# S5 input projections ahead of their blocks, stored in their final layout, and four MLA gates in the last heads

## The chip, the cores and the metric

One core of one Trainium2 chip runs the whole program. The metric is the device time of one execution in microseconds (us). TensorE multiplies matrices, VectorE (DVE) and GpSimd (POOL) compute elementwise, ScalarE (ACT) evacuates and casts, and SyncE (SP) issues every DMA of this kernel. Each engine works through its own queue strictly in order and waits there on semaphores of the others.

## What is computed

The reference runs two decoder layers over 512 tokens of width 1024 in float32. Each layer normalises its input, projects it once, runs three causal mixers on slices of that projection, and merges them by gates:

```python
h = rms_norm(x, g_pre)
p = h @ w_in       # SSD z, x/B/C, dt | S5 input u, gate z_b | MLA q latent, kv latent, rope key, gate z_c | 3 merge gates
A = ssd_branch(...) @ w_a       # Mamba-2 SSD in chunks of 128
B = s5_branch(...) @ w_b        # complex diagonal SSM, 64 groups of 16 channels, state 64
C = mla_branch(...) @ w_c       # 16 heads, q rank 512, kv rank 256, rotary key
merged = sum(sigmoid(gate_i) * branch_i)
x = x + rms_norm(merged @ w_o, g_post)
```

The S5 branch takes u = the S5 slice of p, 1024 channels by 512 tokens, through

```python
bu = einsum('gph,bsgh->bsgp', bb, uf)            # input matrix per group
x  = associative_scan(complex_combine, (abar, bu))
y  = Re(einsum(c, x)) + d_skip * uf
```

## The kernel before

Activations are held transposed, channels on the partitions and the 512 tokens in the free dimension. Every float32 product is made of three matmuls of split operands (upper times upper, lower times upper, upper times lower). `dense` (L108) does one projection of 128 output channels: `weight` (L92) loads a 512 KB tile wf on SP (L102, two buffers), ScalarE casts it to its upper half wh (L66), VectorE or, in the MLA stage for every third tile, POOL subtracts to get the lower half wl (L78, L81), and 24 matmuls of 128x512 follow (L116, L117, L119). `proj` is `dense` on a tile of w_in; UB + b is the S5 input of block b, GT + 8 * i + m the merge gate of branch i, tile m.

A layer (`layer`, L980) has two stages. In the MLA stage (`mla`) the latents are projected and normalised (`normed`, with row sums and copies through TensorE, L231 and L237, and a power on POOL that gives rs_r), and a loop over 16 heads makes queries, keys and values for the heads ahead (`make_q`, `make_k`, `make_v`), scores of head h + 1 (`attend_qk`) and the values of head h. `make_k` also copies the rotary parts of queries, qh and ql, by DMA (L550). Beside it runs the preparation of S5, a Python generator (`s5_prep`) that `fill(n)` advances by n steps after each head: 2 after even heads, 3 after odd ones, one after each of two points near the latents.

`s5_prep` goes through eight blocks of eight groups. `block(b)` projects the block, ScalarE evacuates it with the tokens reversed inside their eights (L321), SP stores it to DRAM (ud, L322), loads it back in eight pieces so that 128 partitions hold offset and channel (puf, L325), and stores that again as u2 (printed as u, L329), for the S5 stage later. `front(b, s)` makes the filters of two groups on POOL (pv, pw, and a store odr, L365); `back(b, s)`, one step later, transposes pw (pm, L377), multiplies it with the split input (pM, L386 and L387), makes pk from pv (L395) and stores kpad (L404) and, at the end of the block, the chunk sums mo (msd, L406). The tiles pu, puf and pmo share one tag with two buffers.

In the mix stage (`mix`) two gates of branch 2 are made, the attention outputs are scaled by rows copied with a selector (L1014, L1026) and split, and eight merges of the MLA branch (one gate and one product with w_c each, gates two ahead) run beside `s5_scan`, 63 sequential steps of four small VectorE operations (L896 to L899). Then come the SSD part, the S5 blocks and the output.

The order on each engine is not written by hand: the program is handed to a scheduler that takes the order in which the code is written as priority, fits instructions into each engine's queue by its own timeline and may pull them forward where their operands and buffers allow.

## Time and profile before

| | us |
|---|---|
| median of 3 runs | 1980.36 |
| lowest, highest | 1975.66, 1982.38 |
| the profiled execution | 1977.92 |
| its span | 1976.1 |
| TensorE busy in it | 1870.3 (95%) |
| VectorE busy | 1420.3 (72%) |
| ScalarE busy | 914.2 (46%) |
| POOL busy | 631.9 (32%) |

In layer 0 the MLA stage runs from about 25 to 390 us, mix from there to about 1025; in layer 1 the MLA stage runs from about 1045 to 1366. The engine shares are means over stages with different limits, so the tables of stretches are read before them. "Idle" is the time for which an engine stood before an instruction, with the instruction that released it. The granted clock is a share of TensorE's full 2.4 GHz; 0.5 is its lower level, 1.2 GHz.

### The profile page before, as it was taken

What the parts mean: (1) busy time and instruction counts of PE and PEld (TensorE: products, weight loads), DVE (VectorE), ACT (ScalarE), POOL (GpSimd) and SP (SyncE); (2) the same over time, 40 slices, a digit from 0 to 9 for tenths busy, and PEclk for the clock granted to TensorE, in tenths of its full rate; (3) what the DMA queues carried; (4) which work ended last, traced back from release to release, by engine and by line L of the source; (5) the groups of instructions that cost most, each with busy time, mean ns of one, the idle gap of its engine ahead of it and who ended that gap; (6) DMA issues with size and microseconds to landing.
All of it is one profiled execution on the core that took longest, in us unless ns stands there. A gap on an engine that the chain in (4) does not pass through costs nothing.

```text
span 1976.1 us, 28153 instructions
## 1 busy us (share of the span) xinstructions
PE 1870.3 (95%) x9880; PEld 1528.1 (77%) x9880; DVE 1420.3 (72%) x2882; ACT 914.2 (46%) x1647; POOL 631.9 (32%) x679
## 2 busy tenths in 40 slices
PE   7898999899999989999998989999999999999998
PEld 5687777687877868888876877776878887788887
DVE  6866566799999857744578566667999996776443
ACT  4355455522555545533332555554235663554331
POOL 1746656201233201201118465661013331012010
PEclk9898998899999999999997999998999999999999
DMA  5343333322321266345233334343332224662541
GB/s 158 94 114 94 108 114 103 119 92 84 128 65 64 75 187 182 92 152 167 90 83 90 111 93 122 100 128 96 96 130 75 74 76 113 183 174 86 171 128 43
DMA packets 136253, 219.99 MB, mean 111 GB/s; under 512 B 39856, under 2 KB 79408, under 8 KB 135600
## 3 DMA queue, kind: packets, MB, share of 16 engines
q1 hardware_dynamic: 136112, 218.19, 37.1%
q8 instruction: 78, 1.28, 0.3%
q14 instruction: 63, 0.52, 0.1%
HBM read 182.08 MB, written 31.33 MB: 108 GB/s over the span
## 4 chain that ended last, share of the span: by engine, by line
PE 60%; DVE 22%; DMA 9%; ACT 3%; issue 2%; POOL 2%; SPq 2%; DVEq 0%; ACTq 0%; POOLq 0%
PE mm L116 15%; PE mm L117 14%; PE mm L119 14%; DMA wf<-in_w_in 3%; DVE wl L78 3%; DVE keep L69 3%; PE mm L61 2%; PE mm L62 2%; PE mm L63 2%; PE aux L61 1%; DVE tmp L69 1%; DVE ms L899 1%; PE aux L62 1%; PE aux L63 1%; DVE sc_t L896 1%
## 5 line engine op out<-in xcount | busy, mean ns | idle before, releaser
L116 PE MATMUL mm<-hh,wh 128*128 128x512 f32 (+1 forms) x1232 | 499.5, 405 | 11.5 <-ACT wh L66 8.0
L66 ACT ACTIVATE wh<-wf 128x1024 fp32r<-128x1024 f32 (+1 forms) x294 | 291.3, 994 | 440.2 <-PE mm L117 227.2
L117 PE MATMUL mm<-hl,wh 128*128 128x512 f32 (+1 forms) x1232 | 492.0, 399 | 0.0
L78 DVE TENSOR_TENSOR wl<-wf,wh 128x1024 fp32r<-128x1024 f32 (+1 forms) x243 | 294.8, 1218 | 188.1 <-ACT wh L66 154.3
L119 PE MATMUL mm<-hh,wl 128*128 128x512 f32 (+1 forms) x1232 | 314.9, 393 | 1.9 <-DVE wl L78 1.9
L116 PEld LDWEIGHTS mm<-hh,wh 128*128 128x128 f32 (+1 forms) x1232 | 236.5, 192 | 72.2 <-ACT wh L66 11.6
L117 PEld LDWEIGHTS mm<-hl,wh 128*128 128x128 f32 (+1 forms) x1232 | 236.2, 192 | 48.5 <-issue 0.5
L119 PEld LDWEIGHTS mm<-hh,wl 128*128 128x128 f32 (+1 forms) x1232 | 228.2, 188 | 52.6 <-DVE wl L78 2.3
L81 POOL TENSOR_TENSOR mg<-mg,tmp 128x512 f32<-128x512 f32 x32 | 77.7, 2431 | 458.1 <-DVE tmp L78 240.5
L81 POOL TENSOR_TENSOR wl<-wf,wh 128x1024 fp32r<-128x1024 f32 (+1 forms) x51 | 108.9, 2135 | 302.6 <-PE mm L119 209.3
L116 PE MATMUL mm<-ah,wh 128*128 128x512 f32 x512 | 200.3, 393 | 0.0
L117 PE MATMUL mm<-al,wh 128*128 128x512 f32 x512 | 199.9, 391 | 0.0
L119 PE MATMUL mm<-ah,wl 128*128 128x512 f32 x512 | 127.6, 390 | 0.0
L116 PEld LDWEIGHTS mm<-ah,wh 128*128 128x128 f32 x512 | 96.2, 188 | 21.4 <-ACT pkf L66 0.7
L117 PEld LDWEIGHTS mm<-al,wh 128*128 128x128 f32 x512 | 96.1, 188 | 20.9 <-issue 1.0
L119 PEld LDWEIGHTS mm<-ah,wl 128*128 128x128 f32 x512 | 95.7, 188 | 19.6
L617 DVE CUSTOM_DVE_ANT_0 sc<-aux,cmask 128x128 f32<-128x128 f32 (+3 forms) x128 | 60.9, 485 | 63.5 <-PE aux L63 62.5
L66 ACT ACTIVATE sc<-sc,nm 128x128 f32<-128x128 f32 (+3 forms) x128 | 70.4, 554 | 13.3 <-DVE nm L73 13.2
L81 POOL TENSOR_TENSOR pv<-pq,ar 128x288 f32<-128x288 f32 x64 | 49.1, 789 | 77.2 <-PE pk L395 68.7
L69 DVE SCALAR_TENSOR_TENSOR keep<-mm,cw,keep 128x511 f32<-128x511 f32 (+2 forms) x96 | 71.1, 740 | 2.0 <-ACT keep L66 1.5
L66 ACT ACTIVATE tmp<-mm 128x512 f32<-128x512 f32 x76 | 44.8, 592 | 56.2 <-PE mm L63 31.5
L81 POOL TENSOR_TENSOR pw<-pbb,ar 128x256 f32<-128x256 f32 x64 | 51.0, 799 | 41.8 <-PE pm L377 41.6
(346 smaller groups left out, 4002.8 us busy)
## 6 DMA issues: line engine op xcount, KB each, us to landing
wf<-in_w_in SPq DMA_DIRECT2D x156, 512.0 KB, 3.6
odr<-pv SPq DMA_DIRECT2D x64, 128.0 KB, 2.0
wf<-in_w_c SPq DMA_DIRECT2D x16, 512.0 KB, 3.4
wf<-in_w_a SPq DMA_DIRECT2D x16, 512.0 KB
wf<-kpad SPq DMA_DIRECT2D x128, 64.0 KB, 6.4
wf<-odr SPq DMA_DIRECT2D x16, 512.0 KB, 7.1
wf<-in_w_glu SPq DMA_DIRECT2D x16, 512.0 KB, 3.4
wf<-in_w_b SPq DMA_DIRECT2D x16, 512.0 KB, 3.8
```

Of the source, the lines that this page charges most:

```text
L61: mm(out, ah, bh, start=start, stop=False)
L62: mm(out, ah, bl, start=False, stop=False)
L63: mm(out, al, bh, start=False, stop=stop)
L66: self.nc.scalar.activation(out, in_, func, **kw)
L69: self.nc.vector.scalar_tensor_tensor(out, in0, s, in1, op0, op1)
L78: self.nc.vector.tensor_tensor(out, a, b, op)
L81: self.nc.gpsimd.tensor_tensor(out, a, b, op)
L116: mm(ps[:m], wh[:, o(i)], bh, start=i == 0, stop=False)
L117: mm(ps[:m], wh[:, o(i)], bl, start=False, stop=False)
L119: mm(ps[:m], wl[:, o(i)], bh, start=False, stop=i == k - 1)
L617: nc.vector.tensor_tensor_reduce(out=sc, in0=ps[:, :n], in1=self.cmask[:, 512 - n:512], op0=ALU.add, op1=ALU.max, scale=1.0, scalar=-3.0e3 ...
L896: nc.vector.tensor_tensor(t1, sc1, s, ALU.mult)
```

## The change

The S5 projection becomes a function of its own, `s5_u`, with the evacuation and eight stores that put the tile in DRAM in the layout u2, in runs of 64 floats. Two blocks are projected right behind the latents (`inputs(2)`), one in each odd head behind `make_k` and `make_v`. In `s5_prep` the block is no longer projected; `load(b)` fetches it with one load (puf, now L328) together with three small loads of its matrices, one quarter of a block ahead. pu, puf and pmo get tags of their own. There is one step less per block, so `fill` is 2 after every head. The first four gates of branch 2 are made in heads 12 to 15, into four buffers of a tag gk, for which a smaller `dynamic_dma_scratch_size` leaves the space; the call in `mix` then finds them made.

```diff
+    def s5_u(self, l, pp, b):
+
+        ps = self.proj(l, UB + b)
+        u = pp.tile([P, 512], F32, name="pu", tag="pu").rearrange("p (j c) -> p j c", j=8)
+        self.act_(u[:, ::-1], ps.rearrange("p (c j) -> p j c", j=8))
+        for g in range(8):
+            self.nc.sync.dma_start(
+                self.u2[b, :, 64 * g:64 * g + 64].rearrange("(j h) c -> h j c", j=8), u[16 * g:16 * g + 16],
+            )
...
-        def block(b):
-
-            ps = self.proj(l, UB + b)
-            u = pf("pu").rearrange("p (j c) -> p j c", j=8)
-            self.act_(u[:, ::-1], ps.rearrange("p (c j) -> p j c", j=8))
-            nc.sync.dma_start(ud[b].rearrange("g h j c -> (g h) j c"), u)
-            uf = pf("puf")
-            for j in range(8):
-                nc.sync.dma_start(
-                    uf[16 * j:16 * j + 16].rearrange("h (g c) -> h g c", g=8),
-                    ud[b, :, :, j].rearrange("g h c -> h g c"),
-                )
-            nc.sync.dma_start(u2[b], uf)
+        def load(b):
+
+            uf = pt("puf", [P, 512], 2)
+            nc.sync.dma_start(uf, u2[b])
             g8 = slice(8 * b, 8 * b + 8)
-            x1, x2 = (pt(n, [P, 8, 2, 16]) for n in ("bc1", "bc2"))
+            x1, x2 = pt("bc1", [P, 8, 2, 16]), pt("bc2", [P, 8, 2, 16], 2)
...
-                keep["mo"] = pf("pmo").rearrange("p (g c) -> p g c", g=8)
+                keep["mo"] = pt("pmo", [P, 512], 2).rearrange("p (g c) -> p g c", g=8)
...
-        todo = None
+        todo, nxt = None, load(0)
         for b in range(8):
-            blk = block(b)
-            yield
+            blk = block(b, *nxt)
             for s in range(4):
...
+                if s == 2 and b < 7:
+                    nxt = load(b + 1)
                 yield
...
-        t = self.tmp()
+        t = self.tp.tile([P, 512], F32, name="gk", tag="gk", bufs=4) if i == 2 and m < 4 else self.tmp()
...
             cq, ckv = latent(CQ, 4), latent(CKV, 2)
+            inputs(2)
             cq = normed(*cq, qn, "cq")
...
+                if h % 2 == 1:
+                    inputs(1)
                 if h < 15:
                     pr[h + 1] = self.attend_qk(mp, q[h + 1], kt[(h + 1) % 2], h + 1)
                 values(h)
-                fill(3 if h % 2 else 2)
+                self.gates_ahead(l, 2, max(0, h - 11))
+                fill(2)
...
-            self.gates, self.gdone = {}, [0, 0, 0]
-            self.gates_ahead(l, 2, 2)
+            self.gates_ahead(l, 2, 4)
...
-    nc = bacc.Bacc("TRN2", target_bir_lowering=False, num_devices=1)
+    nc = bacc.Bacc("TRN2", target_bir_lowering=False, num_devices=1, dynamic_dma_scratch_size=1024)
```

What this does to the order on the engines is shown at three places. The first is SP's queue near heads 4 and 5 of layer 0, before the change: the round trip of block 2 (puf, u), the copies qh and ql, the stores of the block before (kpad, msd) and of the filters (odr), and the weight load of a projection (wf).

```order
L325 DMA puf<-ud_582 16x8x64 x8
L550 DMA qh<-rrh 32x512
L550 DMA ql<-rrl 32x512
L550 DMA qh<-rrh 32x512
L550 DMA ql<-rrl 32x512
L329 DMA u_581<-puf 128x512
L404 DMA kpad_578<-pkf 16x128 x4
L406 DMA msd_580<-pmo 2x64x512
L365 DMA odr_579<-pv_2144 128x2x128 x2
L102 DMA wf<-in_w_in 128x1024
```

The same place in the changed program:

```order
L246 DMA u_393<-pu 16x8x64 x8
L102 DMA wf<-in_w_ukv 128x512
L557 DMA qh<-rrh 32x512 x2
L557 DMA ql<-rrl 32x512 x2
L328 DMA puf<-u_393 128x512
L102 DMA wf<-in_w_in 128x1024 x2
L409 DMA kpad_579<-pkf 16x128 x4
```

The weight loads now stand ahead of the stores of kpad and odr, and behind the eight stores of the tile and one reload.

The second place is POOL's queue in the prologue of layer 0, before the change: the last instructions ahead of rs_r, which the normalisation of the q latent waits for (pw and pv are filter products, pbs and pu factors of them, wl the lower half of a weight).

```order
L81 TENSOR_TENSOR pw_1183<-pbb_766,ar 128x256
L81 TENSOR_TENSOR pw_1193<-pbb_766,ar 128x256
L81 TENSOR_TENSOR wl<-wf,wh 128x1024
L81 TENSOR_TENSOR pv_1334<-bc_815,ai 128x288
L81 TENSOR_TENSOR pbs<-pbs,pu_819 128x128
L81 TENSOR_TENSOR rs_r<-rs_v,mhalf 128x4
```

The last instructions ahead of rs_r in the changed program:

```order
L81 TENSOR_TENSOR pw_1261<-pbs,ai 128x256
L81 TENSOR_TENSOR pv_1259<-bc_854,ai 128x288
L81 TENSOR_TENSOR pv_1258<-pv_1258,pv_1259 128x288
L81 TENSOR_TENSOR pv_1421<-bc_854,ai 128x288
L81 TENSOR_TENSOR pv_1258<-pv_1258,pv_1421 128x288
L81 TENSOR_TENSOR pu_1443<-bc_1297,p_fis 128x128
L81 TENSOR_TENSOR rs_r<-rs_v,mhalf 128x4
```

Counted from the first product with p_fr, 15 instructions of POOL stood ahead of rs_r, and now stand 24, among them the filters of a whole further quarter block and no lower half of a weight.

The third place is TensorE's queue at the seam of MLA and mix in layer 0, before the change: copies with the selector (aux from r2 and sel), the third gate (mm_4651 from hh) and the first merge (mm_4619 from al).

```order
L119 MATMUL mm_4651<-hh_110,wl_4647 128x512 x3
L1026 MATMUL aux_4331<-r2_4287,sel_4294 128x512
L119 MATMUL mm_4651<-hh_110,wl_4647 128x512 x3
L1026 MATMUL aux_4338<-r2_4287,sel_4294 128x512
L119 MATMUL mm_4651<-hh_110,wl_4647 128x512 x2
L117 MATMUL mm_4619<-al_4300,wh_4614 128x512
```

The same place in the changed program, where mm_4676 and mm_4708 are the first two merges:

```order
L1044 MATMUL aux_4381<-r2_4344,sel_4351 128x512
L116 MATMUL mm_4676<-ah_4356,wh_4671 128x512
L116 MATMUL mm_4708<-ah_4356,wh_4703 128x512
L1044 MATMUL aux_4388<-r2_4344,sel_4351 128x512
L117 MATMUL mm_4676<-al_4357,wh_4671 128x512
```

The gate between the copies is gone, and matmuls of the first two merges stand there.

## Rows read from the trace of the kernel before

All rows are of the one profiled execution; times are microseconds from the start of its span.

**Rows 1.** Busy time of each engine in four stretches: the two MLA stages without their ends (105 to 360 and 1085 to 1340), and in layer 0 the first part of the mix stage (402 to 480) and the SSD part (480 to 700). Columns: stretch, its length, then busy us and instructions of PE, PEld, DVE, ACT and POOL, then the granted TensorE clock as a share of full speed, the DMA share and GB/s.
```profile
105.00:360.00 255.00, 237.81 (x1329) 197.79 (x1328) 159.45 (x359) 139.93 (x331) 146.18 (x200) 0.94 0.37 109
...
402.00:480.00 78.00, 78.00 (x351) 63.85 (x349) 74.97 (x259) 18.96 (x23) 4.79 (x2) 1.00 0.30 95
480.00:700.00 220.00, 213.49 (x1137) 173.09 (x1136) 197.31 (x326) 115.11 (x187) 64.36 (x44) 0.98 0.28 86
1085.00:1340.00 255.00, 239.14 (x1341) 198.00 (x1341) 159.68 (x361) 139.70 (x332) 153.97 (x206) 0.95 0.39 110
```

**Rows 2.** The same view for the stretches in the two MLA stages in which the granted clock falls to about half.
```profile
181.00:191.00 10.00, 6.66 (x26) 5.61 (x26) 6.77 (x14) 6.03 (x14) 7.59 (x12) 0.51 0.36 113
325.00:335.00 10.00, 9.26 (x30) 7.62 (x31) 8.11 (x20) 4.97 (x11) 6.71 (x12) 0.51 0.40 125
...
1126.00:1130.00 4.00, 3.94 (x12) 2.91 (x12) 1.76 (x6) 3.28 (x11) 0.00 (x0) 0.58 0.59 185
1167.00:1174.00 7.00, 4.18 (x16) 3.52 (x17) 5.88 (x14) 4.46 (x11) 6.35 (x10) 0.55 0.32 94
1307.00:1314.00 7.00, 6.32 (x24) 5.10 (x24) 6.01 (x16) 3.58 (x8) 3.19 (x7) 0.54 0.45 125
```

**Rows 3.** The timeline of TensorE at the places where it stood idle in the MLA stages. Columns: start, duration, engine, line, operation, tiles and shape, and in brackets the idle time just before, with what ended it.
```profile
183.68 0.69 PE L377 MATMUL pm<-ident,pw 128*128 128x128 f32 x2 [3.68 <-ACT pkf L66]
...
241.84 0.33 PE L61 MATMUL aux<-kh,qh 96*128 96x128 f32 x1 [3.38 <-DMA qh<-rrh]
...
325.27 0.47 PE L386 MATMUL pM<-pu,pmh 128*128 128x128 f32 x1 [1.57 <-ACT pmh L66]
...
1124.84 0.33 PE L386 MATMUL pM<-pu,pmh 128*128 128x128 f32 x1 [1.84 <-DVE pu L78]
...
1168.61 0.66 PE L377 MATMUL pm<-ident,pw 128*128 128x128 f32 x2 [2.41 <-ACT pkf L66]
...
1305.60 0.33 PE L386 MATMUL pM<-pu,pmh 128*128 128x128 f32 x1 [2.56 <-ACT pmh L66]
```

**Rows 4.** The timeline of ScalarE at the casts of a weight tile into its upper half (the same columns).
```profile
182.13 1.06 ACT L66 ACTIVATE wh<-wf 128x1024 fp32r<-128x1024 f32 x1 [4.68 <-DMA wf<-in_w_in]
...
322.58 1.06 ACT L66 ACTIVATE wh<-wf 128x1024 fp32r<-128x1024 f32 x1 [1.55 <-DMA wf<-in_w_in]
...
1302.91 1.06 ACT L66 ACTIVATE wh<-wf 128x1024 fp32r<-128x1024 f32 x1 [1.90 <-DMA wf<-in_w_in]
```

**Rows 5.** The timeline of SP's queue ahead of the weight load whose cast is the first row of group 4. The durations are the time that SP takes to issue.
```profile
169.41 0.46 SPq L329 DMA_DIRECT2D u<-puf  x1
169.92 1.84 SPq L404 DMA_DIRECT2D kpad<-pkf  x4
171.81 0.57 SPq L406 DMA_DIRECT2D msd<-pmo  x1
172.47 0.93 SPq L365 DMA_DIRECT2D odr<-pv  x2
173.51 1.10 SPq L102 DMA_DIRECT2D wf<-in_w_in  x1
```

**Rows 6.** The list of DMA issues of the whole program: how many, KB each, and the median us from issue to landing.
```profile
wf<-in_w_in SPq DMA_DIRECT2D x156, 512.0 KB, 3.6
...
odr<-pv SPq DMA_DIRECT2D x64, 128.0 KB, 2.0
...
puf<-ud SPq DMA_DIRECT2D x128, 32.0 KB, 2.0
```

**Rows 7.** The timeline of SP's queue ahead of the copies of head 8's query.
```profile
234.43 0.41 SPq L322 DMA_DIRECT2D ud<-pu  x1
...
237.05 2.71 SPq L325 DMA_DIRECT2D puf<-ud  x6
...
239.86 1.20 SPq L550 DMA_DIRECT2D qh<-rrh  x2
```

**Rows 8.** The prologue of the two MLA stages: timeline rows of POOL (from the first product with p_fr to rs_r in layer 0, the first product in layer 1), timeline rows of PE (the row sums and copies of L237 in both layers, and two later waits in layer 1), and last the page's group of the filter products pv (busy us, mean ns of one, idle before).
```profile
62.77 1.45 POOL L81 TENSOR_TENSOR pbb<-bc,p_fr 128x128 f32<-128x128 f32 x1 [2.18 <-DVE p_fr L78]
...
74.50 1.02 POOL L81 TENSOR_TENSOR rs_r<-rs_v,mhalf 128x4 f32<-128x4 f32 x1
...
1047.72 0.46 POOL L81 TENSOR_TENSOR pbb<-bc,p_fr 128x128 f32<-128x128 f32 x1 [1.78 <-DVE p_fr L78]
...
78.61 1.94 PE L237 MATMUL aux<-tmp,ones 128*128 128x512 f32 x2 [3.44 <-DVE tmp L73]
...
1056.19 1.13 PE L237 MATMUL aux<-tmp,ones 128*128 128x512 f32 x2 [1.83 <-DVE tmp L73]
...
1062.94 0.69 PE L377 MATMUL pm<-ident,pw 128*128 128x128 f32 x2 [2.86 <-POOL pw L81]
...
1079.39 0.42 PE L387 MATMUL pM<-pu,pml 128*128 128x64 f32 x1 [4.22 <-DVE pml L78]
...
L81 POOL TENSOR_TENSOR pv<-pq,ar 128x288 f32<-128x288 f32 x64 | 49.1, 789 | 77.2 <-PE pk L395 68.7
```

**Rows 9.** Groups of VectorE's instructions from 395 to 450 us: one of the four operations of a scan step (busy us, mean ns of one, idle before).
```profile
L899 DVE TENSOR_TENSOR ms<-ms,sc_t 128x64 f32<-128x64 f32 x37 | 10.4, 282 | 0.9
```

**Rows 10.** The timeline of TensorE at the seam of MLA and mix in layer 0: the last copy with the selector and the first matmul of the gate after the first two merges.
```profile
390.54 0.50 PE L1026 MATMUL aux<-r,sel 64*128 64x512 f32 x1
...
401.89 0.39 PE L116 MATMUL mm<-hh,wh 128*128 128x512 f32 x1
```

More of the change, by code (lines that the diff above doesn't have):

```diff
@@ L303, in s5_prep @@
         d = lambda nm, shape: self.dr.tile(shape, F32, name=f"{nm}{l}")
-        kpad, odr, msd, u2 = d("kpad", [16, 64, 240]), d("odr", [P, 64, P]), d("msd", [2, 64, 2, 32, 64]), d("u2", [8, P, 512])
-        ud = d("ud", [8, 8, 16, 8, 64])
+        kpad, odr, msd, u2 = d("kpad", [16, 64, 240]), d("odr", [P, 64, P]), d("msd", [2, 64, 2, 32, 64]), self.u2
         nc.sync.dma_start(kpad[:, :, 0:112], zero.unsqueeze(1).broadcast_to([16, 64, 112]))
@@ L310, in s5_prep @@
         et = self.gt
-        pf = lambda nm: pp.tile([P, 512], F32, name=nm, tag="pf", bufs=2)
         bbp = [pt(f"pbb{i}", [P, 8, 32]) for i in range(2)]
@@ L334, in block @@
             nc.sync.dma_start(x2[64:128], a["s5_bc"][l, 0:64, g8])
+            return uf, x1, x2
+        def block(b, uf, x1, x2):
+            g8 = slice(8 * b, 8 * b + 8)
             b1, b2, c1, c2 = x1[:, :, 0], x2[:, :, 0], x1[:, :, 1], x2[:, :, 1]
             fb = lambda x: x[:, g8].unsqueeze(2).broadcast_to([P, 8, 16])
-            u1, bs, q1 = (pt(n, [P, 8, 16]) for n in ("pu1", "pbs", "pq1"))
+            u1 = pp.tile([P, 8, 16], F32, name="pu1", tag="pv2")
+            bs, q1 = (pt(n, [P, 8, 16]) for n in ("pbs", "pq1"))
             bb = bbp[b % 2][:, :, 0:16]
@@ L478, in merge, with mla @@
         self.gt(mg, mg, g, ALU.add)
-    def mla(self, l, fill):
+    def mla(self, l, fill, inputs):
         nc, tc, a = self.nc, self.tc, self.a
@@ L987, in layer, with inputs @@
         self.yc = []
+        self.gates, self.gdone = {}, [0, 0, 0]
         with ExitStack() as pst:
             pp = pst.enter_context(tc.tile_pool(name=f"prep{l}", bufs=1, reuse_waits="tile", side="right"))
+            self.u2 = self.dr.tile([8, P, 512], F32, name=f"u2{l}")
+            todo_u = list(range(8))
+            def inputs(n):
+                for b in todo_u[:n]:
+                    self.s5_u(l, pp, b)
+                del todo_u[:n]
             prep = self.s5_prep(l, pp)
@@ L994, in fill @@
                     next(prep, None)
-            self.mla(l, fill)
+            self.mla(l, fill, inputs)
             fill(99)
```

## Prediction

> **What bounds the kernel now.** I read the table of stretches first, because the share of busy time over the whole program hides that its stages have different limits. In the MLA stage TensorE has matmuls in flight for 237.81 of 255 us in layer 0 and 239.14 of 255 in layer 1, at a granted clock of 0.94 and 0.95, while VectorE is busy 159 us and SP's queue moves data at a share of 0.37 to 0.39 [rows 1]. So TensorE sets the pace there, and what is lost is lost in two ways: it stands still, or it runs at 1.2 instead of 2.4 GHz after it stood still. In the first part of the mix stage (402 to 480 us) TensorE is never idle and VectorE is busy 74.97 of 78 us; in the SSD part (480 to 700) TensorE has 6.5 us free and VectorE 22.7 [rows 1]. VectorE has slack in MLA, little in mix.
>
> Then I looked for the places where the clock falls, and what TensorE waited for just ahead of them. At 181 to 191 us the granted clock is 0.51, at 325 to 335 again 0.51, and in layer 1 0.58 at 1126, 0.55 at 1167, 0.54 at 1307 [rows 2]. Ahead of them TensorE idles for 3.68, 1.57, 1.84, 2.41 and 2.56 us [rows 3], in four of the five for ScalarE, in whose queue the cast of a weight tile is waiting: the row of that cast at 182.13 had idled 4.68 us for the DMA of its weights, the one at 322.58 1.55 us, the one at 1302.91 1.90 us [rows 4]. SP shows why the weights were late: their issue at 173.51 stands behind the S5 store at 169.41, four kpad stores, the msd store and two odr stores, which SP issues first [rows 5]. From that issue to the cast are 182.13 - 173.51 = 8.6 us, although such a transfer takes 3.6 at the median [rows 4 to 6]: the weights are issued late, and then travel behind what was issued ahead of them. The S5 round trip through DRAM (ud out, eight puf in, u out) thus costs little itself; what costs is that it and the stores of the block before stand in SP's strictly ordered queue in front of weights.
>
> **The change part by part.** TensorE executes the same number of matmuls. What goes are 16 ud stores, 128 puf loads and 16 u stores; what comes are 128 stores of the evacuated tile and 16 reloads, and each tile is stored a head or more ahead of its use.
>
> *Late weights (gain).* In the changed order weights, the copies and the reload follow on the S5 stores, and kpad and odr come behind them. Each place costs its idle time plus what the low clock loses: at 181 us 3.68 + 10 x (1 - 0.51) = 8.6; at 1167 2.41 + 7 x 0.45 = 5.6; at 325 1.57 + 4.9 = 6.5; at 1307 2.56 + 7 x 0.46 = 5.8 [rows 2, 3]. All together 26.5 us. The first two hang on the queue order that goes, and I take them whole (14.2). At the other two the weights' own wait is shorter (1.55 and 1.90), and with it gone the next thing in ScalarE's queue can be late too, so I take half (6.1). Sum 20.3 us, bounds 7 and 26.5.
>
> *Late S5 input (gain).* At 1124.84 the pM matmuls wait 1.84 us for the split of the reloaded input, and 4 us at 0.58 follow [rows 2, 3]: 1.84 + 1.7 = 3.5 us. The reload now goes out one quarter of a block ahead of the block's first use, from data stored long before. I take 3.5, bounds 0 and 3.5.
>
> *Query copies behind more issues (loss).* Head 8's copies (idle of 3.38 us at 241.84 [rows 3]) were issued 239.86 - 234.43 = 5.4 us after the ud store [rows 7]. Now eight stores stand there, at 2.71 / 6 = 0.45 us per issue 3.6 us, then the landing of the last store (2.0 as for odr, also a store of short pieces [rows 6]; the weight load behind it is issued in its shadow) and the reload (0.46 [rows 5]): 6.1 us, or 0.7 later. With as much at a lowered clock that is about 1 us in each layer: 2 us, bounds 0 and what the rival below gives. A 256 B-piece store to DRAM has no row here; the nearest are the 256 B loads and the 512 B odr stores, both 2.0 [rows 6].
>
> *Prologue.* The normalisation of the q latent needs rs_r from POOL, which runs in order. Before, rs_r starts at 74.50, behind POOL work that began with p_fr's product at 62.77, and TensorE's row 78.61 follows 3.1 us after rs_r ends, having idled 3.44 [rows 8]. In the changed order 24 POOL instructions, from that product on, stand ahead of it: 15 of 0.79 and 8 of 0.46 are 15.5 us [rows 8], near 17 with a square over 512 columns, so rs_r would start near 80.0, 5.5 later. The second S5 projection at the latents is 24 matmuls more ahead of that point, 5.3 us by the rows' 0.222 (78 us with 351 matmuls [rows 1]). The two cancel: the idle time stays near 3.6. In layer 1 the same 17 us after 1047.72 give 1064.7 for rs_r and 1069 for the row that was at 1056.19: 12.8 later, with 5.3 of cover and thus 7.5 us more idle time. Against that, TensorE's waits of 2.86 us for pw and 4.22 for pml [rows 8] fall away, as POOL has by then gone through these filters. I charge 2 us, bounds a gain of 3 and a loss of 8.
>
> *Two projections per layer from mix into MLA.* One more S5 projection at the latents and one more gate in heads 12 to 15 (two of the four gates already ran in heads 13 and 14, since the scheduler had pulled them there). For TensorE alone that is neutral: 10.7 us more in one stage and 10.7 less in the other. But VectorE's scan of 252 small operations (0.28 us each [rows 9]) is worked off beside mix's projections, about 16 operations for each. At the start of SSD 89 of them are left in the order before and 106 after: 17 x 0.27 = 4.7 us more VectorE work there per layer, with 22.7 us free in 220 [rows 1]. I take half, 2.3 per layer, so 4.7 us; bounds 0 and, if nothing of the removed 10.7 us comes out of mix, 21.
>
> *Seam between MLA and mix.* Gate 2's matmuls stood between the eight sel copies. The last copy is at 390.54 and the next gate at 401.89 [rows 10], 11.4 us, which is the two merges in between (2 x 5.3) and hardly more. Without gate 2, the copies are paced by VectorE's multiplication and split, so that they end hardly earlier while 5.3 us of cover are gone; the merges fill it in part, as the order shows. I charge 1 us per layer, 2 us; bounds a gain of 3 and a loss of 6.
>
> Sum: 20.3 + 3.5 - 2 - 2 - 4.7 - 2 = 13.1 us off. The profiled execution took 1977.92 us (a span of 1976.1 and 1.8 around it), which gives 1964.8. The median of the runs lies 2.4 above that execution, so I forecast **1967 us**.
>
> **The rivals.** *All stalls go.* The late weights at their upper bound, 26.5, the late input 3.5, the 3.38 us idle time at 241.84 with about 1.7 at a lowered clock also gone (5), prologue and seam at their gains (3 + 3), nothing lost on VectorE: 41 us off, 1937, or 1939 by the median. For it speaks that all these waits have SP's queue behind them; against it that the prologue's waits are POOL's and that VectorE has little slack in mix.
>
> *The stalls only move.* With weights early, the copies or ScalarE's evacuations can be the next to be late, at the same places. Then half of the 14.2 us remains, 7, against the losses of 10.7: 3.7 slower than the profiled run, 1982 and 1984 by the median, which is no change. *The two projections are paid twice:* VectorE keeps mix as long as it is (74.97 of 78 busy) while MLA grows by 2 x 10.7 = 21. Then 23.8 - 21 - 6 = -3, also 1984 by the median. The free 22.7 us in the SSD part speak against it.
>
> *Slower: the short-piece stores.* The reload puf waits for the last of eight stores, and SP holds everything behind it: copies at heads 8 and 12, in both layers four places. If a store takes 2.0 us to land, the cost is the 2 us above. Beyond that each further microsecond is idle time at four places, and a stretch at the low clock comes on top, at 1167 us 7 x 0.45 = 3.2 [rows 2]. From about 3.5 us of landing it decides: each place then loses 1.5 + 3.2 us, and 4 x 4.7 = 19 against 13 is the bound to slower. At the full price of the place at 181 us, 8.6 us each, it is 34 - 13 = 21 us slower: 1999; the middle of the two is 27, 1977.9 - 13.1 + 27 + 2.4 = 1994. For it speaks that the pieces are half as long as odr's; against it the puf loads, which have 256 B pieces and land in 2.0 [rows 6].
>
> The Trainium skill (DMA: Bandwidth & Descriptors, Specifications) says that line rate needs transfers of at least 512 B and that shorter ones make the engines read, modify and write. By that the stores would be the slow ones and the 1994 of this rival the forecast. No run here shows a 256 B store, and the 256 B loads landing in 2.0 agree with no such loss on the reading side.
>
> That the change doesn't do what it says is excluded: the built order has the second projection at the latents and the gates in the last heads.
>
> **How the numbers follow.** A measurement of this kernel can tell about 0.3% from no change, 6 us, so faster is under 1974.4 and slower over 1986.3. The forecast (1955 to 1974) gets 0.43, all stalls gone 0.12, stalls moved 0.17, paid twice 0.10, short-piece stores 0.18. Faster is 0.43 + 0.12 = 0.55, the same 0.27, slower 0.18. The range reaches from the upper part of the all-gone case, 1942, to the lower half of the store rival, 1990; what lies outside is about half of either, 0.15.
>
> **What would show it.** Right: no wait of over 3 us for weights in ScalarE's casts near heads 4 and 12, a clock of 0.97 or more over the MLA stretches, and MLA longer by less than 10.7 us per layer while the mix stage is shorter by 5 to 10. Wrong: SP waiting for u2 stores longer than 2.5 us with TensorE idle for copies behind it; rs_r late in layer 1 with TensorE idle for over 8 us; VectorE over 95% busy in the SSD part with TensorE waiting for it; or idle times of the same sum that name other releasers.

## The result and the profile after

| | us |
|---|---|
| after, median of 4 runs (1998.40 to 2002.53) | 2001.51 |
| before, beside it, median of 4 runs (1975.66 to 1982.38) | 1978.69 |
| ratio, with its 95% interval | 1.0120 (1.0099 to 1.0141) |
| span of the profiled execution, before and after | 1976.1 and 2000.4 |

The kernel became slower by some 23 us, where a gain was forecast. The range of 1942 to 1990 does not hold the time.

Where the 24.3 us of the two spans lie is seen by three marks in each layer, read from the timelines: TensorE's first score matmul (aux from kh, qh), its last copy with the selector, and SP's first load of w_o. Differences are taken before rounding.

| from, to | before | after | difference | of it, moved work | rest |
|---|---|---|---|---|---|
| layer 0: start to first score | 111.7 | 119.6 | +7.9 | +5.3 | +2.6 |
| first score to last copy | 278.8 | 282.8 | +4.0 | 0 | +4.0 |
| last copy to w_o | 476.7 | 476.7 | 0 | -5.3 | +5.3 |
| layer 1: w_o to first score | 224.9 | 232.4 | +7.5 | +5.3 | +2.2 |
| first score to last copy | 277.5 | 280.7 | +3.3 | 0 | +3.3 |
| last copy to w_o | 469.8 | 471.7 | +1.9 | -5.3 | +7.2 |

What moved is one S5 projection from the heads to the latents, and the third and fourth gate out of the seam and the mix stage into the heads (5.3 us each by the forecast's 0.222 us for a matmul). So the heads get one projection less and one gate more than they and the seam had together, and mix one gate less. The rests are 4.8 us in the prologues, 7.2 in heads and seam, 12.5 in mix.

The same stretches as in [rows 1], after:

```profile
105.00:360.00 255.00, 233.55 (x1280) 195.21 (x1281) 163.30 (x353) 134.33 (x318) 152.43 (x203) 0.93 0.36 100
402.00:480.00 78.00, 78.00 (x350) 63.34 (x350) 74.43 (x269) 19.36 (x22) 4.85 (x2) 1.00 0.28 88
480.00:700.00 220.00, 209.50 (x1117) 169.50 (x1115) 195.59 (x349) 112.26 (x183) 64.50 (x43) 0.99 0.25 80
1085.00:1340.00 255.00, 231.40 (x1271) 192.00 (x1271) 169.15 (x361) 135.27 (x321) 157.58 (x211) 0.93 0.35 97
```

The MLA stretches have less TensorE work in them than before and no better clock (0.93 against 0.94 and 0.95). The idle times of [rows 3] are gone from their places, and others stand elsewhere. TensorE's timeline after:

```profile
86.88 1.12 PE L237 MATMUL aux<-tmp,ones 128*128 128x512 f32 x2 [3.15 <-DVE tmp L73]
...
181.52 0.47 PE L61 MATMUL aux<-kh,qh 96*128 96x128 f32 x1 [4.47 <-DMA qh<-rrh]
...
395.42 0.79 PE L1044 MATMUL aux<-r,sel 64*128 64x512 f32 x1 [3.88 <-DVE keep L78]
...
1096.90 0.48 PE L391 MATMUL pM<-pu,pmh 128*128 128x128 f32 x1 [6.04 <-ACT pmh L66]
...
1175.39 0.47 PE L61 MATMUL aux<-kh,qh 96*128 96x128 f32 x1 [4.20 <-DMA qh<-rrh]
```

The low clock follows them as it did the old ones:

```profile
180.00:187.00 7.00, 5.48 (x25) 4.69 (x25) 1.61 (x6) 1.01 (x2) 0.23 (x1) 0.52 0.51 174
388.00:402.00 14.00, 8.00 (x16) 4.24 (x17) 9.67 (x24) 4.64 (x9) 0.00 (x0) 0.64 0.54 175
1173.00:1180.00 7.00, 4.61 (x22) 3.77 (x22) 0.69 (x1) 1.01 (x2) 1.57 (x3) 0.53 0.67 198
```

ScalarE still waits for weights. These are its waits for the loads of weight tiles in the stretches 105 to 360 and 1085 to 1340 us (total, times, longest), after:

```profile
ACT wh L66 <- DMA wf<-in_w_in: 9.5, 4, 4.5
ACT wh L66 <- DMA wf<-in_w_ukv: 5.6, 1, 5.6
...
ACT wh L66 <- DMA wf<-in_w_in: 6.9, 2, 4.5
ACT wh L66 <- DMA wf<-in_w_ukv: 5.6, 2, 5.2
ACT wh L66 <- DMA wf<-in_w_uq: 1.8, 1, 1.8
```

And before:

```profile
ACT wh L66 <- DMA wf<-in_w_in: 7.5, 3, 4.7
ACT wh L66 <- DMA wf<-in_w_uq: 1.0, 1, 1.0
...
ACT wh L66 <- DMA wf<-in_w_in: 6.0, 2, 4.1
ACT wh L66 <- DMA wf<-in_w_uq: 6.0, 1, 6.0
```

That is 29.4 us after and 20.5 before. Two of the casts after:

```profile
181.30 0.63 ACT L66 ACTIVATE wh<-wf 128x512 fp32r<-128x512 f32 x1 [5.62 <-DMA wf<-in_w_ukv]
...
297.96 1.06 ACT L66 ACTIVATE wh<-wf 128x1024 fp32r<-128x1024 f32 x1 [4.46 <-DMA wf<-in_w_in]
```

The load for the second one was issued 2.70 us behind an msd store, and its cast began 6.89 us after its issue, where such loads land in 3.5 us at the median:

```profile
288.37 0.57 SPq L411 DMA_DIRECT2D msd<-pmo  x1
290.47 0.38 SPq L370 DMA_DIRECT2D odr<-pv  x1
291.07 0.33 SPq L102 DMA_DIRECT2D wf<-in_w_in  x1
```

The place at 181 us can be followed back. SP's queue ahead of the copies that TensorE waited for:

```profile
163.94 0.57 SPq L411 DMA_DIRECT2D msd<-pmo  x1
165.32 1.72 SPq L409 DMA_DIRECT2D kpad<-pkf  x4
167.15 0.38 SPq L370 DMA_DIRECT2D odr<-pv  x1
172.65 0.36 SPq L331 DMA_DIRECT2D bc<-in_s_bc  x1
173.05 0.53 SPq L332 DMA_DIRECT2D bc<-in_s_bc  x1
173.64 0.59 SPq L333 DMA_DIRECT2D bc<-in_s_bc  x1
174.33 3.88 SPq L246 DMA_DIRECT2D u<-pu  x8
178.33 0.36 SPq L102 DMA_DIRECT2D wf<-in_w_ukv  x1
```

SP issues nothing from 167.5 to 172.65; the load bc of L331, whose tile has one buffer, waits for POOL, which has to have read the tile's last content. POOL's timeline at that time:

```profile
165.34 0.47 POOL L81 TENSOR_TENSOR pbb<-pbb,pu 128x128 f32<-128x128 f32 x1
171.93 0.11 POOL L378 MEMSET pmo<- 128x8 f32 x1 [6.12 <-DMA msd<-pmo]
172.00 0.62 POOL L81 TENSOR_TENSOR pu<-bc,p_fi 128x128 f32<-128x128 f32 x1
```

POOL stands 6.12 us ahead of a memset of 0.11 us, until the msd store that was issued at 163.94 has landed, 8 us later. Then pu frees bc, SP loads it, issues the eight stores for 3.88 us, and only then the copies. Over layer 0's MLA stage that memset's group reads, after and before:

```profile
L378 POOL MEMSET pmo<- 128x8 f32 x6 | 0.7, 112 | 31.1 <-DMA msd<-pmo 25.4 <-DVE mx L627 5.7
```
```profile
L373 POOL MEMSET pmo<- 128x8 f32 x7 | 0.8, 113 | 6.9 <-DMA msd<-pmo 4.7 <-DMA wf<-in_w_uq 1.8 <-DMA kpad<-pkf 0.4
```

And SP's waits for POOL's filters, ahead of the odr stores, rose from the second row's value to the first's (total, times, longest):

```profile
SPq L370 <- POOL pv L81: 67.8, 19, 7.9
```
```profile
SPq L365 <- POOL pv L81: 26.8, 13, 8.5
```

The tag of its own is what let the scheduler pull the memset up to the store of the block that had used the tile. At the seam VectorE stands for a small load that now lies behind the last msd store in SP's queue, and the copies with the selector behind VectorE:

```profile
394.61 0.17 DVE L75 TENSOR_SCALAR e_zc<-alog 128x16 f32<-128x16 f32 x1 [3.61 <-DMA alog<-in_a_log]
```

### The profile page after: what moved, and what is told of

Its sections match the earlier page's. It is cut to its first block, busy times and chain, and to the rows that moved or that the text cites. A ratio compares the mean times of both kernels' runs of the same rounds, so it can differ in the third digit from the quotient of the medians.

```text
span 2000.4 us, 28062 instructions
## 1 busy us (share of the span) xinstructions
PE 1872.1 (94%) x9880; PEld 1531.8 (77%) x9880; DVE 1413.7 (71%) x2882; ACT 913.6 (46%) x1647; POOL 632.1 (32%) x679
## 4 chain that ended last, share of the span: by engine, by line
PE 54%; DVE 22%; DMA 13%; ACT 3%; issue 3%; SPq 3%; POOL 2%; DVEq 0%; ACTq 0%; POOLq 0%
PE mm L116 13%; PE mm L117 13%; PE mm L119 11%; DVE wl L78 4%; DVE keep L69 3%; DMA msd<-pmo 2%; PE mm L61 2%; DMA wf<-in_w_in 2%; PE mm L63 2%; PE mm L62 2%; DVE sc_t L906 2%; DVE ms L909 2%; DMA wf<-odr 2%; PE aux L61 2%; ACT wh L66 1%
## 5 line engine op out<-in xcount | busy, mean ns | idle before, releaser
L116 PE MATMUL mm<-hh,wh 128*128 128x512 f32 (+1 forms) x1232 | 493.2, 400 | 10.5 <-DVE keep L69 8.9
L78 DVE TENSOR_TENSOR wl<-wf,wh 128x1024 fp32r<-128x1024 f32 (+1 forms) x243 | 302.2, 1247 | 203.3 <-ACT wh L66 143.8
L119 PE MATMUL mm<-hh,wl 128*128 128x512 f32 (+1 forms) x1232 | 320.3, 394 | 3.1 <-DVE wl L78 3.1
L116 PEld LDWEIGHTS mm<-ah,wh 128*128 128x128 f32 x512 | 97.8, 191 | 24.2 <-ACT ah L66 4.2
L119 PEld LDWEIGHTS mm<-ah,wl 128*128 128x128 f32 x512 | 97.8, 191 | 20.9 <-issue 0.5
L61 PE MATMUL aux<-kh,qh 96*128 96x128 f32 (+3 forms) x128 | 46.2, 377 | 19.4 <-DMA qh<-rrh 9.9
L66 ACT ACTIVATE tmp<-mm 128x512 f32<-128x512 f32 x68 | 40.1, 594 | 51.5 <-PE mm L63 31.8
```

Of the source, the lines that this page charges most:

```text
L61: mm(out, ah, bh, start=start, stop=False)
L66: self.nc.scalar.activation(out, in_, func, **kw)
L78: self.nc.vector.tensor_tensor(out, a, b, op)
L116: mm(ps[:m], wh[:, o(i)], bh, start=i == 0, stop=False)
L119: mm(ps[:m], wl[:, o(i)], bh, start=False, stop=i == k - 1)
```

## The experiments

Kernels that ran beside the same runs of the kernel before are compared by their medians, others by their ratios to it.

**The two parts alone.** e1 keeps the S5 part:

```diff
-        t = self.tp.tile([P, 512], F32, name="gk", tag="gk", bufs=4) if i == 2 and m < 4 else self.tmp()
+        t = self.tmp()
...
-                self.gates_ahead(l, 2, max(0, h - 11))
...
-            self.gates_ahead(l, 2, 4)
+            self.gates_ahead(l, 2, 2)
```

> The S5 part alone: inputs ahead and stored in final layout as in the changed kernel; the gates of branch 2 made where they were before the change. Theory (scan): the gates taken out of the mix stage leave VectorE's scan with less TensorE work beside it, scan steps run into the SSD part (in the order 44 and 46 scan operations stand behind the first convolution operation of layer 0 and 1 in the changed kernel, 25 and 18 before the change, 16 and 5 here), and this is worth some 13 us of the 23: 1988, with the mix stages of both layers as short as before. Rival (stores): the eight short-piece stores make copies and weights late; then it stays near 2001, with the same waits for qh in MLA. Rival (prologue): 2001 as well, with the later rs_r unchanged.

Measured 1987.89, ratio 1.0057 (1.0041 to 1.0073). The gates cost 0.0120 - 0.0057, some 12 us; the S5 part alone still loses.

e2 adds only the gates to the kernel before, with the same three edits the other way round and the smaller DMA scratch:

> The gates part alone on the kernel before: four gates of branch 2 in heads 12 to 15, S5 inputs as before. Theory (scan): 1992, some 13 over the kernel before, because 64 and 58 scan operations stand behind the first convolution operation. Rivals (stores, prologue): no loss without the S5 part, 1979 within 6.

2031.20, ratio 1.0284 (1.0255 to 1.0313): a far larger loss than expected. In its profile the last msd store is issued at 396.13 instead of 379.63, the chunk sums load at 403.89 instead of 387.50, and the scan starts at 411.65, where before it did at 396.62. The gates push the end of the S5 preparation back and the scan with it, and from the last copy to w_o it takes 500.0 and 485.0 us in the two layers, 38.5 more than before. In the whole change, the three come at 385.75, 393.59 and 401.77.

**The stores.** e3 stores the tile once into the intermediate layout and makes the short loads in `load(b)`:

```diff
-        for g in range(8):
-            self.nc.sync.dma_start(
-                self.u2[b, :, 64 * g:64 * g + 64].rearrange("(j h) c -> h j c", j=8), u[16 * g:16 * g + 16],
-            )
+        self.nc.sync.dma_start(self.ud[b].rearrange("g h j c -> (g h) j c"), u)
...
-            nc.sync.dma_start(uf, u2[b])
+            for j in range(8):
+                nc.sync.dma_start(
+                    uf[16 * j:16 * j + 16].rearrange("h (g c) -> h g c", g=8),
+                    self.ud[b, :, :, j].rearrange("g h c -> h g c"),
+                )
+            nc.sync.dma_start(u2[b], uf)
```

> The changed kernel with S5 inputs projected as far ahead, but stored once into the intermediate layout in 2 KB pieces; load(b) makes the eight short loads and the u2 store of the kernel before. Rival (stores): if the 256 B-piece stores cost the time, it is faster than the changed kernel by some 10: 1991. Theory (scan): the same 2001 within 6.

2027.98, ratio 1.0262 (1.0244 to 1.0279). Without the short stores it is 26 us slower than with them, so the rival's forecast fails. The edit also puts eight loads and a store into every `load(b)`, and does not isolate the stores; their landing is read further down. The same copies are waited for longer:

```profile
1179.56 0.48 PE L61 MATMUL aux<-kh,qh 96*128 96x128 f32 x1 [6.12 <-DMA qh<-rrh]
```

**How far ahead.** e4:

```diff
-            inputs(2)
+            inputs(1)
...
-                if h % 2 == 1:
+                if h % 2 == 0:
                     inputs(1)
```

> The changed kernel with one S5 input at the latents instead of two, and one in each even head instead of each odd one. rs_r then stands at the same place of POOL's queue as before the change. Rival (prologue): it gives back the 5 us by which the prologues lost more, 1996, with a shorter idle time ahead of the row sums' copies (3.15 and 4.38 in the changed kernel). Theory (scan): 2001 within 4, as the scan's order is the same.

2034.64, ratio 1.0301 (1.0279 to 1.0323). The first scores come at 113.8 us instead of 119.6, so the prologue gives back what was expected; but from there to the last copy layer 0 takes over 20 us more than in the changed kernel, with 55.5 us of SP's waits for wl and 13.8 of u stores that wait behind ScalarE's other work. The edit moved the losses and does not isolate the prologue.

**The memset.** e5:

```diff
+        mos = [pt(f"pmo{i}", [P, 512]).rearrange("p (g c) -> p g c", g=8) for i in range(2)]
+        for t in mos:
+            nc.gpsimd.memset(t[:, :, 0], 0.0)
...
-                keep["mo"] = pt("pmo", [P, 512], 2).rearrange("p (g c) -> p g c", g=8)
-                nc.gpsimd.memset(keep["mo"][:, :, 0], 0.0)
+                keep["mo"] = mos[b % 2]
```

> The changed kernel with two fixed tiles for the chunk sums pmo, whose zero column is set once, instead of a fresh tile and memset in every block. Theory (memset): with a tag of its own the memset was pulled right behind the msd store of the block that had the buffer; POOL stands 4 to 6 us there in each block (31 us in layer 0, 6.9 before the change), pv and the odr stores come late, SP waits for them (67.8 us in layer 0, 26.8 before) and holds copies and weights. Then the waits of SP for pv fall to 30 or less, the idle times of 4.47 and 4.20 us for qh go, and the time is 1992. Rival (moves): the stalls go to the next late thing, 2001 within 4.

1992.00, ratio 1.0063 (1.0041 to 1.0084), as expected. The idle time for qh shrinks to 2.69 us and 2.56 us, but does not go; SP's waits for pv fall only to 51.3 us, so that part of the chain was overstated.

```profile
176.36 0.33 PE L61 MATMUL aux<-kh,qh 96*128 96x128 f32 x1 [2.69 <-DMA qh<-rrh]
```
```profile
SPq L373 <- POOL pv L81: 51.3, 13, 8.0
```

The same on the kernel before, e12 giving pmo its tag and e15 the fixed tiles (both with the smaller DMA scratch):

```diff
-                keep["mo"] = pf("pmo").rearrange("p (g c) -> p g c", g=8)
+                keep["mo"] = pt("pmo", [P, 512], 2).rearrange("p (g c) -> p g c", g=8)
```

> The kernel before with one line changed: pmo gets a tag of its own with two buffers, as in the change (and the smaller DMA scratch that leaves the space). Theory (memset): the memset is pulled forward to the msd store and POOL stands there in each block: 1985 to 1990. Rival: the memset harms only with the input's reload next to it, 1979 within 5.

1992.66, ratio 1.0090 (1.0068 to 1.0113), a larger loss than expected. With that line alone the memset's idle time is as long as in the changed kernel:

```profile
L373 POOL MEMSET pmo<- 128x8 f32 x6 | 0.7, 113 | 32.4 <-DMA msd<-pmo 16.3 <-DVE ql L78 6.0 <-DVE pml L78 5.8
```

> The kernel before with the zero column set once in two fixed tiles (and the smaller DMA scratch), so that pu and puf alone share the tag. Theory (memset): it waited 6.9 us in layer 0 already, a gain of 2 to 6: 1972. Rival: 1976, the waits were covered.

1983.54, ratio 1.0038 (1.0018 to 1.0059). Against e12, which has the same tags for the rest, the repeated memset costs 0.0052, some 10 us, with intervals that do not meet. Against the kernel before, there is no gain but a loss of some 7 us, against the expectation. It lies in mix (480.4 and 474.1 us from the last copy to w_o, some 4 more in each layer than before), and its cause stays open: pu and puf have the shared tag to themselves, and the DMA scratch is smaller. No run has the smaller scratch alone; e16 below has it and is level with the kernel before.

**The seam.** e6 moves the loads of dtb and alog to the layer's start (e7 is e1 with this and the fixed tiles, e8 e5 with this):

```diff
         self.krdt = self.sm.tile([64, 512], F32, name="krdt")
+        bias, al = self.sm.tile([P, 16], F32, name="dtb"), self.sm.tile([P, 16], F32, name="alog")
+        nc.sync.dma_start(bias, a["dt_bias"][l:l + 1, :].broadcast_to([P, 16]))
+        nc.sync.dma_start(al, a["a_log"][l:l + 1, :].broadcast_to([P, 16]))
+        self.dtal = bias, al
...
+        bias, al = self.dtal
```

> The changed kernel with the two small loads of ssd_dt (dtb, alog) issued at the start of the layer. Theory (seam): they were issued behind the last msd store, VectorE stood 3.61 and 3.28 us at the first operation on alog, and TensorE's copies with the selector stood 3.88 and 3.25 behind it, at half the clock; 8 us less, 1994. Rival: the copies are paced by the multiplications and splits anyway, and the scan by the load of the chunk sums: 2001 within 3.

> The S5 part alone (gates where they were before the change) with both repairs, the zero column set once and the small loads early. If memset and seam are what the S5 part loses, it is at or under the kernel before: 1974. Rival: the S5 part has other losses (prologue, moved stalls) and stays at 1988.

> The whole change with both repairs. If both add up, 1985; what then stays over the kernel before is the scan's share of the gates and the prologue. If the scan's theory is wrong, 1977 or less.

2021.22, 2003.22 and 2009.91 (ratios 1.0220, 1.0124, 1.0167): each 17 to 21 us over its counterpart without the edit (the changed kernel, e10 and e5) by the ratios. VectorE stood for the next small load instead, and SP stood for tiles that the layer before still used; whether these two make up the whole loss is not shown:

```profile
395.81 0.20 DVE L73 TENSOR_SCALAR cw<-cw 128x64 f32<-128x64 f32 x1 [4.83 <-DMA cw<-in_conv_w]
```
```profile
SPq L995 <- DVE d_x L78: 10.3, 1, 10.3
```

e9 (on e5) and e11 (on e10, below) give all six small loads, early, tiles for each layer:

```diff
+        ct = lambda nm, shape: self.const.tile(shape, F32, name=f"{nm}_{l}")
+        bias, al, cw, cb = ct("dtb", [P, 16]), ct("alog", [P, 16]), ct("cw", [P, 16, 4]), ct("cb", [P, 16])
+        dsk, sn = ct("dsk", [P, 8]), ct("sn", [P, 8])
...
```

> The changed kernel with the zero column set once and all six small loads of the mix stage (dtb, alog, cw, cb, dsk, sn) early, into tiles of their own for each layer. With only dtb and alog early, VectorE stood 4.83 us for cw at the same place, and SP stood 10.3 us in layer 0 for the loads of layer 1, which had to wait for the tiles of layer 0. Theory (seam): with both waits gone the seam gives 6 to 8 us: 1985. Rival: something else is late at the seam (the chunk sums' load), 1992 within 3.

> The same with all small loads early as well. If the seam costs what its idle time says: 1972, under the kernel before. Rival: 1979.

1990.51 and 1990.02 (ratios 1.0081 and 1.0073): no gain over e5, and a loss of 8.6 us against e10, which ran beside e11. In e9 the stop between the copies is gone:

```profile
384.12 0.93 PE L1048 MATMUL aux<-r,sel 64*128 64x512 f32 x3 [3.14 <-DVE r L78]
385.36 1.39 PE L1048 MATMUL aux<-r,sel 64*128 64x512 f32 x2 [0.31 <-DVE keep L78]
```

From the last score to the last copy it takes 3.5 and 3.6 us less than e5 in the two layers, but from the last copy to w_o 1.0 us less and 6.6 more. The wait was real, and in this profile most of what its removal gave is lost again in layer 1's mix.

**Gates and scan.** e10 is e1 with the fixed tiles of e5. e13 and e14 are e10 and e5 with the scan's loop left out (`range(63)` becomes `range(0)`; the chunk sums pass unscanned).

> The S5 part alone (gates where they were before the change) with the zero column set once. If memset (9.5 us) and gates (13.6) are separate losses, they add: 2001.5 - 9.5 - 13.6 = 1978, the same as the kernel before. Rival: they overlap, both through a late end of the S5 preparation, 1987.

> The S5 part with the zero column set once, gates where they were before the change, with the 252 scan operations of each layer left out (the chunk sums are loaded and stored unscanned). To be read against the next run alone, which differs from it by the gates. Theory (scan): without the scan VectorE has slack in mix; about 1969, and the next run equal within 2.

> The whole change with the zero column set once, with the 252 scan operations of each layer left out in the same way. Theory (scan): the gates cost 10.6 us only because VectorE's scan then sets mix, so without it this is equal to the run before it, within 2, about 1969. Rival: the gates lose in the heads and at the seam (no cover between the selector copies), then it stays 8 to 11 above the run before it.

e10 is 1981.41, ratio 1.0038 (1.0024 to 1.0051): the gates cost 0.0025 on top of it, with intervals that overlap, so here less is certain than the 12 us without the fixed tiles. Without the scan the sign turns: 1973.17 without the gates' move (ratio 0.9986, 0.9956 to 1.0017) and 1965.84 with it (0.9944, 0.9930 to 0.9959), 7.3 us less, with intervals that just overlap. The time from the last copy to the first load of w_o, in the two layers: 482.2 and 469.8 in e10, 476.9 and 472.0 with the gates moved (e5); 474.1 and 468.2 in e13, 465.7 and 458.7 in e14. These two ends in layer 1, of e13 and then of e14:

```profile
1367.38 0.50 PE L1045 MATMUL aux<-r,sel 64*128 64x512 f32 x1
...
1835.57 0.33 SPq L1080 DMA_DIRECT2D wf<-in_w_o  x1
```
```profile
1365.10 0.79 PE L1046 MATMUL aux<-r,sel 64*128 64x512 f32 x1
...
1823.81 0.33 SPq L1081 DMA_DIRECT2D wf<-in_w_o  x1
```

In these single profiles, moving the gates shortens mix by 3.1 us in both layers together beside the scan, and by 17.9 without it. The scan itself gets longer: from its first to its last operation it takes 99.6 and 95.7 us in e10, 106.5 and 108.0 in e5, as it takes 97.1 and 92.8 before the change and 106.2 and 107.5 after.

**The prologue.** e16 is e10 with the second input behind the normalisation:

```diff
-            inputs(2)
+            inputs(1)
             cq = normed(*cq, qn, "cq")
+            inputs(1)
```

> The S5 part with the zero column set once and the gates where they were, with the second S5 input at the latents put behind the normalisation of the q latent instead of ahead of it; 18 instead of 24 instructions of POOL then stand ahead of rs_r. Theory (prologue): TensorE's idle time ahead of the row sums' copies moves behind cover, 2 to 3 us in each layer: 1976. Rival: the projection only changes places with the wait, 1981 within 2.

1974.75, ratio 0.9992 (0.9977 to 1.0007): the S5 part, with both repairs, is level with the kernel before. The ways from the start and from w_o to the first score get 1.2 and 6.1 us shorter than in e10. The idle time that shrinks most is the one further on, in layer 1 from 5.22 us in e10 to 1.08 in e16:

```profile
1089.72 0.47 PE L393 MATMUL pM<-pu,pmh 128*128 128x128 f32 x1 [5.22 <-ACT pmh L66]
```
```profile
1062.86 2.08 PE L237 MATMUL aux<-tmp,ones 128*128 128x512 f32 x2 [4.26 <-DVE tmp L73]
...
1079.38 0.33 PE L393 MATMUL pM<-pu,pmh 128*128 128x128 f32 x1 [1.08 <-ACT pmh L66]
```

Even here ScalarE waits for weights as long as before: 21.0 us in the two MLA stretches against 20.5, and four of its waits, of 4.12 to 4.39 us, are for loads issued 2.7 us behind an msd store, which reach their cast 6.8 to 7.0 us after their issue. One of them:

```profile
293.42 1.06 ACT L66 ACTIVATE wh<-wf 128x1024 fp32r<-128x1024 f32 x1 [4.39 <-DMA wf<-in_w_in]
```

**A lighter scan.** e17 is e16, e18 e5 with e16's edit, both with one operation of each step on POOL:

```diff
-            nc.vector.tensor_tensor(t2, sc2, s[:, ::-1], ALU.mult)
+            nc.gpsimd.tensor_tensor(t2, sc2, s[:, ::-1], ALU.mult)
```

> The S5 part with the zero column set once and the second input behind the normalisation, gates where they were before the change, and one of the four operations of each scan step on POOL, which is busy under 5 of 78 us there. Theory (scan): VectorE loses 17 us of work per layer in the stage where it is full; 1969 if its load counts. Rival: the chain of steps gets longer by the handing over between engines and counts for more: 1980 or above.

> The same with the gates in heads 12 to 15: the whole change with the two repairs and a quarter of the scan on POOL. If the scan's load on VectorE is what makes the gates dear, they cost less than the 10.6 us that they cost with the whole scan on VectorE: 1973, 4 over the run before it. If the length of the chain counts, 10 us or more over it.

1984.64 (ratio 1.0035, 1.0022 to 1.0047) and 2015.97 (1.0197, 1.0180 to 1.0214). With a quarter of the scan's operations off VectorE the gates cost 31 us instead of less; the theory of VectorE's load alone does not hold. VectorE's scan operations also stand for the other engine's result here (idle time 4.6 us at the last operation of the steps in e18, against 1.5 at the same operation in e16). From its first to its last operation the scan takes 97.8 and 99.1 us in e17, no less than the 95.5 and 98.6 in e16, and 107.9 and 105.5 in e18. So the gates' move stretches the scan by 6 to 10 us in each layer here too, and the lighter load did not shorten it; where the rest of the 31 us is lost is not shown.

## Why the prediction was wrong

*Late weights, 20.3 us of gain.* This is the step that failed. The forecast held that weights which stand ahead of kpad and odr in SP's queue come in time, and it priced the first two places whole, as if nothing else could be late there; the rival that the stalls only move was given 0.17. Shown instead: ScalarE's waits for weights did not go. They are 29.4 us in the two MLA stretches, against 20.5 before, with 5.62 us at 181.30, where the first priced place was, and the granted clock is 0.93 in both stretches. In heads and seam 7.2 us were lost.

Two things hold the weights up. At 181 us SP itself stands for POOL, and then issues eight stores ahead of the load. Elsewhere a load goes out close behind an msd store, which the new order left in place: 2.70 us behind it in both layers, and then 6.9 us to the cast. The load at 173.51 of [rows 5], whose 8.6 us the prediction put down to all that was issued ahead of it, went out 1.7 us behind an msd store too. No run moved that store, so this second cause is read from the rows and not tested.

That the gain is missing also without the losses that follow below is seen in e16. From first score to last copy it takes 5.9 and 4.9 us less than the kernel before, and 5.3 of each is the projection that moved to the latents. Of the 23.8 us priced for late weights and late input nothing is left within a microsecond.

The term's sum also counts some idle time twice: 2.68 of the 3.68 us ahead of 183.68 lie inside the stretch from 181 on, whose whole length was priced at the low clock, and likewise 1.61 of the 2.41 us at 1167. That is some 2 us of the 26.5.

*What was not in the sum: the tag.* The part on the change costed the memory of pmo at nothing. The memset of 0.11 us was pulled behind the msd store and stood there in POOL's queue for 31.1 us in layer 0. Shown by e5, e12 and e15: 10 to 11 us of the loss, on the changed kernel and on the one before. The way from POOL's stop through bc and SP to the copies is read from one place of the trace; SP's waits for pv carry little of it, as e5 showed. Along one path of runs the whole loss comes off: the ratio falls from 1.0120 by 0.0057 without the repeated memset (e5), by 0.0025 without the gates' move (e10) and by 0.0046 with the second projection behind the normalisation (e16).

*Late S5 input, 3.5 us of gain.* The wait of [rows 3] for the split input is gone, as forecast, but no run shows time that came back for it.

*Query copies, 2 us of loss.* The mechanism (stores ahead of copies in SP's queue) appeared, but near head 4 and not 8, and with idle times of 4.47 and 4.20 us, at the first of which SP also stood for POOL. The slower rival had such places at heads 8 and 12, but its cause, slow landing of short stores, is refuted by the trace: the stores land in 1.8 us at the median, and SP's reload waits for them 0.9 us at the longest.

```profile
u<-pu SPq DMA_DIRECT2D x128, 32.0 KB, 1.8
```
```profile
SPq L328 <- DMA u<-pu: 8.1, 15, 0.9
```

By the rule of the Trainium skill on transfers under 512 B (DMA: Bandwidth & Descriptors, Specifications) these stores of 256 B pieces would have been the slow ones. The trace does not show that here: they land as fast as the loads of the same pieces did [rows 6].

*Prologue, 2 us of loss.* Mis-sized: 4.8 us are left after the moved projection is taken off. The idle time ahead of the row sums' copies came out near the forecast in layer 0 (3.15 against 3.6) and lower than forecast in layer 1 (4.38 against 9.3); the two waits behind it that were said to fall away are gone by name, but one of 6.04 us for pmh stands there instead. e16, which puts the projection behind the normalisation, is 0.0046 better.

*Two projections into MLA, 4.7 us of loss.* Mis-described and mis-sized. The S5 projection only moved inside the MLA stage; what left seam and mix were gates 2 and 3. The mix stage kept its length (0 and +1.9 us) although it had one gate less, which is the rival "paid twice", given 0.10, at 12.5 of its 21 us. The forecast had the mechanism, scan operations left over beside less TensorE work, at too small a size: the scan takes 9.1 and 14.7 us longer after the change, where 4.7 more of VectorE's work were priced at half. e13 and e14 agree that the scan is what keeps the length. Whether through VectorE's load or through the chain of its dependent steps stays open: e17 and e18 changed both at once.

*Seam, 2 us of loss.* A wait that was not foreseen stood there, VectorE's for alog behind the last msd store. Removed in e9, it gave 3.5 us in each layer up to the last copy, and the time did not fall, which agrees with a stage paced by the scan.

Of the signs that the prediction named, those for "right" did not come: ScalarE has waits of over 3 us for weights, the clock of the MLA stretches is 0.93 and not 0.97, the way from the start or w_o to the last copy is 11.9 and 10.8 us longer, and mix is not shorter. Of those for "wrong", the last came: idle times that name other releasers.

No version that still does the scan was found to beat the kernel before clearly; e16, without the gates' move, is level with it.

## What to carry to other kernels

A tile with a buffer of its own may be written earlier, and a scheduler that fills queues by its own timeline will do so: look in the new order for what a freed instruction now stands behind, above all for a small one that waits for a slow store on an engine that works in order. Before pricing a stall as a gain, follow it to the one thing that ends last: here a new order behind some stores left the weights behind the slow one, and ScalarE waited for them as long at other places. And before work is taken from a stage, ask what runs beside it there: with one gate less beside the serial scan the scan took longer, and the stage was as long as before.

## What the runs showed of the hardware

The msd store, 256 KB with two rows as its outermost dimension, released POOL 8.0 us after its issue (163.94 to 171.93), while 32 KB stores in pieces of 256 B landed in 1.8 us at the median and the copies of query rows in 2.1. The u stores of the kernel before, also 256 KB, took 2.2. Weight loads issued 2.7 us behind an msd store reached their cast 6.8 to 7.0 us after their issue in the changed kernel and in e16, where the median landing of such loads is 3.5 in the changed kernel. Why this store takes so long, and whether it alone delays the loads behind it, no run tests.
